# Three values before the first gates, ten gates beside the block solve, and the decay rows stored later

## The chip, the cores and the metric

The kernel runs on one core of a Trainium2 chip. The time is the device time of one execution in microseconds. Before the change it was 1307.09 us, the median of 3 runs (1301.83 to 1307.75).

A core has five engines with a queue of instructions each, worked off in order: PE (matrix multiply; its weight loads, PEld, overlap), DVE (vector), ACT (activation functions and copies), POOL (general) and SP, which here only issues DMA transfers. ACT issues transfers too, between its other instructions. PE writes its results to PSUM, a small memory of banks, from which ACT or DVE must drain them.

## The reference

One layer of a generator over 256 latent tokens with a prefix of 256 context tokens, width 1024: a half-step FFN, a token mixer, another half-step FFN, a norm. All is float32. The mixer runs two scans in both directions over one normalised input:

```
qkv, za, a, beta, zb, xbc, dt, gates = split(h @ w_in)
q, k, v = silu(conv(qkv));  q, k = l2norm(q), l2norm(k)
gated delta scan (8 heads, chunks of 64), per chunk:
    g = cumsum(log a);  decay = exp(g_i - g_j)
    A = strict_lower((k*beta) k^T * decay) + I;  solve A [u, w] = [v*beta, k*beta*exp(g)]
    o = (q exp(g)) S + (q k^T * decay) (u - w S);  S is updated with (u - w S)
SSD scan (32 heads), per chunk:
    a_cs = cumsum(dt * a_neg);  seg = exp(a_cs_l - a_cs_s), lower part
    y = (C B^T * seg) (x*dt) + C S exp(a_cs);  S is updated
merged = sigmoid(ga) * (ya @ w_branch_gdn) + sigmoid(gb) * (yb @ w_branch_mb)
x = x + m5 * (merged @ w_out)
```

Below, a *key* is one head's slice of k, a *value* one of v, and a *gate* one of 16 tiles of `gates` (ga and gb). The *decay rows* are the a_cs of the SSD scan, laid out as rows.

## The kernel before, in words

**Projections.** A projection in full precision splits its weights: `unit` (L185) loads a 128x1024 tile `raw` (issued on SP, L191), ACT casts it to the high part `whi` (L197), DVE subtracts to get the low part `wlo` (L201), and `mm3` issues three matmuls for each of 8 slices (L212 to L214). Keys and values go this way, with 512 columns (context and latent). Gates need less: `projf` (L643) loads `raw` (L638), and PE multiplies straight from it with 256 latent columns (L648, each issued as two matmuls). Line 27 sets the buffers: four of `raw`, three each of `whi` and `wlo`.

**What follows a projection.** A key or a value goes through `conv_silu` (L651): ACT drains the accumulator into a padded buffer `cbuf` (two, shared by keys and values, L659 to L662) and makes the centre tap (L665), DVE adds the four other taps (L667), ACT takes tanh (L670), DVE finishes (L672). A value is then transposed (L1066), drained by ACT (L1068) and stored (L1069). A key is normalised (`l2`, L919), stored, multiplied with itself (L960) and the product stored as `Gsd` (L963); after keys 1, 3, 5 and 7 its diagonal 32x32 blocks are loaded as `N` (L969, on SP). A gate is drained by one tanh on ACT (L1183) and stored (L1184).

**The solve.** `block_decay` and `row_scale` make the decay factors `D` of the blocks. `elim` (L1041) multiplies `N` by `D` (L1045) and then inverts all 32x32 blocks at once in 30 dependent steps of two DVE instructions each (L1049, L1052). Result and transposed copy (L1058) go to DRAM, and `merge` (L1187) reads them back to build the inverses of whole 128-row tiles on PE, for the chain of scan steps.

**The decay rows.** `dts` (L870) computes the steps dt and their running sums `gc` for the SSD scan, and at its end transposes `gc` (L914), negates it on ACT (L916) and stores the rows as `asd` (L917). The SSD scan's diagonal part (`ssd_diag`, L1471) later loads eight rows at a time, broadcast to 128 partitions (`Es`, L1484, 512 KB each), POOL adds the columns (L1497), and DVE and ACT go on from there.

**Who sets the order.** The parts of the mixer are generators, and `PLAN` (L31) lists which are advanced and by how much. `k6` advances the keys by six, `v2` the values by two, `g5` the gates by five; a word alone calls the method of that name. A number before a slash sets the class from that item on: a lower class is earlier. Classes count up from that number with each instruction, so an item that sets 18 again starts beside the first one that did. A planner then simulates the engines and fills each queue by class among what it believes ready, so an instruction of a late class can stand early where nothing better is ready. Weight loads have a class of their own, earlier than all others, and go in program order.

The two keys 0 and 1 and the small projection for a, beta and dt are multiplied before `PLAN` begins. The merges, the chain's steps, the queries (`q`), the SSD inputs (`x`), the sixteenth gate, the `z` projections and the SSD scan come after what is changed.

Of the kernel before, what the change touches and what calls it, by code (L numbers as in the profile page):

```python
# [27 lines left out]
TAGS = dict(tA=4, tS=3, tL=2, tM=2, tZ=2)  # L28
T4 = 2
NCV = 2  # L30
PLAN = """10/k3 block_decay k6 18/g5 13/dts 20/v2 g3 row_scale 5/elim 20/g7 v7 21/gdn_rows 13/m0 14/m1 13/chain_start s0 s1 m2 m3 22/q9  # L31
    B_part 27/x17 25/lat_h 22/C_part 30/g17 chain_out 13/s2 s3 14/gdn_norm 15/ssd_pre 30/zB1 zA9 zB4 15/h40 51/y0 gdn_out y1 70/mb_out"""
NG = 5
GQ = 0
# [102 lines left out]
class Kernel:  # L137
# [537 lines left out]
    def mixer(self, hg):  # L675
# [29 lines left out]
        self.yb = []  # L705
        for tok in PLAN.split():
            p, _, a = tok.rpartition("/")
# [162 lines left out]
    def dts(self):  # L870

        nc, V = self.nc, self.nc.vector
        C = self.const
        mm = nc.tensor.matmul
        x = self.t2([P, 4, 64], "dtx", tag="tZ")
        e = self.t2([P, 4, 64], "dte", tag="tZ")
        z2 = self.t2([P, 4, 64], "dtz", tag="tL")
        V.tensor_copy(x, self.xdt)
        dt = self.dt = self.xdt
        self.softplus(dt, e, z2, x)  # L880
        g = self.t2([P, 4, 64], "dtg", tag="tL")
        V.tensor_tensor(g, dt, self.alog[:, 16:80].rearrange("p (o c) -> p o c", o=1).to_broadcast([P, 4, 64]), op=ALU.mult)
        pc = self.smp([P, 2, 4, 64], "pcd", "mg")
        for d, tri in enumerate((self.UT, self.LT)):
            mm(pc[:, 0, :, 32 * d:32 * d + 32], tri, g[:, :, 32 * d:32 * d + 32], start=True, stop=True)
        mm(pc[:, 1], self.ones, g, start=True, stop=True)
        gc = self.gc = C([P, 4, 64], "gc")
        V.tensor_copy(gc, pc[:, 0])

        gt = pc[:, 1]  # L890
        wc = self.wc = C([P, 2, 2, 32], "wc")
        for j in range(2):
            for d in range(2):
                t = 2 + j
                cs = slice(32 * d, 32 * d + 32)
                w = wc[:, j, d]
                V.tensor_tensor(w, gt[:, t, cs], gc[:, t, cs], op=ALU.subtract)
                if d == j:
                    V.tensor_tensor(w, w, gt[:, 5 - t, cs], op=ALU.add)
        nc.scalar.activation(wc, wc, AF.Exp)  # L900
        wf = wc.rearrange("p a b c -> p a (b c)")
        V.tensor_tensor(wf, wf, dt[:, 2:4], op=ALU.mult)

        wl, egm = self.wl, self.egm = C([P, 2, 32], "wl"), C([P, 2, 32], "egm")
        for d in range(2):
            cs = slice(32 * d, 32 * d + 32)
            V.tensor_tensor(wl[:, d], gt[:, d, cs], gc[:, d, cs], op=ALU.subtract)
            V.tensor_copy(egm[:, d], gt[:, d, cs])
        nc.scalar.activation(wl, wl, AF.Exp)
        nc.scalar.activation(egm, egm, AF.Exp)  # L910
        for d in range(2):
            V.tensor_tensor(wl[:, d], wl[:, d], dt[:, d, 32 * d:32 * d + 32], op=ALU.mult)
        pr = self.smp([P, P], "prow", "mg")
        nc.tensor.transpose(pr, gc[:, 0:2].rearrange("p t c -> p (t c)"), self.ident)  # L914
        rw = self.t2([P, P], "rows_a", tag="tL")
        nc.scalar.activation(rw, pr, AF.Copy, scale=-1.0)  # L916
        nc.scalar.dma_start(self.asd, rw)  # L917
# [783 lines left out]
```

## Time and profile before

| | |
|---|---|
| median of the runs | 1307.09 us |
| the profiled execution | 1309.47 us, its span 1307.8 us |
| PE busy | 1257.8 us (96%) |
| DVE busy | 950.8 us (73%) |
| ACT busy | 482.2 us (37%) |
| POOL busy | 96.7 us (7%) |
| mean granted PE clock | 0.973 |
| keys, from 420 to 471 us | PE busy 51.00, DVE 50.26 |
| until the solve, 470 to 514 us | PE busy 38.35, DVE 16.85 |
| the solve, 514 to 585 us | PE busy 68.05, DVE 63.48 |

How to read the rows that follow. All times are in microseconds from the span's start, and only "mean" and the figure after a group's busy time are nanoseconds. A row in order of time gives start, duration, engine, line, operation, output and inputs, how many were merged into the row, and in brackets the time that the engine had been idle and what ended the idle time. A queue's name with a q (SPq, ACTq) marks the issue of a transfer. A row of a stretch gives its length and the busy time of each engine with the count of instructions, then the granted clock of PE, the busy share of the DMA engines, and GB/s. A group row gives the busy time of all instructions of one line, the mean, and the idle time ahead of them.

### The profile page before, as it was taken

The numbers are of one execution on the slowest core, as the hardware profiler recorded it, in microseconds if no ns is written. First come the engines' busy times: TensorE is split into PE (matmuls) and PEld (weight loads), VectorE is DVE, ScalarE is ACT, GpSimd is POOL, SyncE is SP. The second block draws the span as 40 slices with busy tenths as digits, with TensorE's granted clock in tenths as the row PEclk, the third lists the DMA queues.
The fourth block names the chain that finished last, engine by engine and source line by source line (L and its number), as shares of the span: only waits on it lengthen the run. The fifth ranks groups of instructions, "written<-read, shape, count | busy, mean of one in ns | idle before, by whom it ended". The sixth has DMA issues, their size and how long they took to land.

```text
span 1307.8 us, 21034 instructions
## 1 busy us (share of the span) xinstructions
PE 1257.8 (96%) x8042; PEld 1096.2 (84%) x8042; DVE 950.8 (73%) x1748; ACT 482.2 (37%) x919; POOL 96.7 (7%) x119
## 2 busy tenths in 40 slices
PE   9999999999999989987999999999997999999997
PEld 8888888888899878877888899868555999999997
DVE  5997686556568964897669799847896566856655
ACT  4322122212236652254323445421223445633333
POOL 1000000000010131001110211100211002000000
PEclk9999999999999999998889999999987999999998
DMA  9566467547532389648434356568645665655552
GB/s 367 183 212 206 129 221 230 192 147 238 181 123 89 105 220 232 212 145 235 108 103 117 122 177 196 175 194 286 219 168 199 193 201 182 192 192 185 186 179 79
DMA packets 138131, 239.40 MB, mean 183 GB/s; under 512 B 41072, under 2 KB 81456, under 8 KB 137904
## 3 DMA queue, kind: packets, MB, share of 16 engines
q1 hardware_dynamic: 98688, 214.32, 51.5%
q10 hardware_dynamic: 39344, 23.76, 6.1%
q8 instruction: 63, 1.03, 0.3%
q14 instruction: 36, 0.29, 0.1%
HBM read 211.72 MB, written 26.31 MB: 182 GB/s over the span
## 4 chain that ended last, share of the span: by engine, by line
PE 65%; issue 16%; DVE 9%; DMA 8%; ACT 1%; SPq 0%; POOL 0%; ACTq 0%; DVEq 0%; POOLq 0%
PE acc L213 16%; PE acc L212 16%; PE acc L214 16%; PE acc L648 4%; DVE Es L1499 1%; PE pSs L1125 1%; PE acc L1161 1%; PE pada L318 1%; DMA raw<-in_wgs 1%; DVE Es L1510 1%; DVE wlo L201 1%; PE pn L1339 1%; DMA zsc<-zbt 1%; PE pP L1330 1%; DMA Lm<-Gsd 1%
## 5 line engine op out<-in xcount | busy, mean ns | idle before, releaser
L197 ACT CAST whi<-raw 128x1024 fp32r<-128x1024 f32 (+1 forms) x208 | 214.5, 1034 | 460.3 <-PE acc L213 350.8
L213 PE MATMUL acc<-hL,whi 128*128 128x512 f32 (+1 forms) x976 | 346.1, 355 | 0.5 <-DVE hL L468 0.5
L214 PE MATMUL acc<-hH,wlo 128*128 128x512 f32 (+1 forms) x976 | 346.5, 355 | 0.0
L212 PE MATMUL acc<-hH,whi 128*128 128x512 f32 (+1 forms) x976 | 342.4, 357 | 0.8 <-ACT cv L665 0.5
L201 DVE TENSOR_TENSOR wlo<-raw,whi 128x1024 fp32r<-128x1024 f32 (+1 forms) x208 | 249.7, 1202 | 80.0 <-ACT whi L197 78.8
L212 PEld LDWEIGHTS acc<-hH,whi 128*128 128x128 f32 x976 | 187.7, 193 | 24.6 <-ACT cv L665 0.7
L213 PEld LDWEIGHTS acc<-hL,whi 128*128 128x128 f32 x976 | 188.1, 193 | 23.9 <-DVE hL L468 0.9
L214 PEld LDWEIGHTS acc<-hH,wlo 128*128 128x128 f32 x976 | 188.0, 193 | 23.4
L290 DVE CUSTOM_DVE_ANT_0 junk<-wadat,cs 128x1024 f32<-128x1024 f32 x80 | 97.7, 1221 | 44.1 <-DMA wadat<-in_wadaT 43.4
L213 PE MATMUL acc<-aL,whi 128*128 128x256 f32 (+1 forms) x384 | 122.9, 323 | 0.0
L214 PE MATMUL acc<-aH,wlo 128*128 128x256 f32 (+1 forms) x384 | 122.3, 323 | 0.0
L212 PE MATMUL acc<-aH,whi 128*128 128x256 f32 (+1 forms) x384 | 122.2, 323 | 0.0
L667 DVE SCALAR_TENSOR_TENSOR cv<-cbuf,cc,cv 128x512 f32<-128x512 f32 (+1 forms) x144 | 97.5, 688 | 16.8 <-ACT cv L665 15.4
L648 PE MATMUL acc<-hF,raw 128*128 128x256 f32 x416 | 97.2, 390 | 7.0 <-ACT gth L1183 7.0
L648 PEld LDWEIGHTS acc<-hF,raw 128*128 128x128 f32 x416 | 80.7, 197 | 21.0 <-ACT gth L1183 7.6
L213 PEld LDWEIGHTS acc<-aL,whi 128*128 128x128 f32 x384 | 73.0, 190 | 5.6
L214 PEld LDWEIGHTS acc<-aH,wlo 128*128 128x128 f32 x384 | 72.7, 190 | 5.6
L212 PEld LDWEIGHTS acc<-aH,whi 128*128 128x128 f32 x384 | 72.6, 190 | 5.7
L604 DVE SCALAR_TENSOR_TENSOR xl<-acc,hg,xl 128x256 f32<-128x256 f32 x64 | 30.3, 481 | 47.6 <-PE acc L214 47.0
L1161 PE MATMUL acc<-raw,hF 128*128 128x512 f32 x128 | 58.6, 610 | 0.0
L1161 PEld LDWEIGHTS acc<-raw,hF 128*128 128x128 f32 x128 | 24.9, 197 | 30.0 <-issue 29.9
L401 POOL TENSOR_TENSOR sqa<-sqa,sqb 128x256 f32<-128x256 f32 x12 | 11.7, 978 | 454.9 <-ACT sqb L399 451.9
(403 smaller groups left out, 1968.4 us busy)
## 6 DMA issues: line engine op xcount, KB each, us to landing
raw<-in_wgu SPq DMA_DIRECT2D x76, 512.0 KB, 4.2
wadat<-in_wadaT SPq DMA_DIRECT2D x56, 512.0 KB, 4.1
raw<-in_wdn SPq DMA_DIRECT2D x44, 512.0 KB, 3.8
wada<-in_wada SPq DMA_DIRECT2D x16, 512.0 KB, 9.6
raw<-in_wg SPq DMA_DIRECT2D x16, 512.0 KB, 3.7
Es<-asd SPq DMA_DIRECT2D x16, 512.0 KB, 4.7
raw<-in_wxs SPq DMA_DIRECT2D x16, 512.0 KB, 4.3
raw<-in_wzB SPq DMA_DIRECT2D x16, 512.0 KB, 3.8
```

Of the source, the lines that this page charges most:

```text
L197: nc.scalar.copy(hi, raw)
L201: engs[i % len(engs)].tensor_tensor(lo[:, c:c + w], raw[:, c:c + w], hi[:, c:c + w].bitcast(F32), op=ALU.subtract)
L212: mm(acc, wh, xh, start=start, stop=False)
L213: mm(acc, wh, xl, start=False, stop=False)
L214: mm(acc, wl, xh, start=False, stop=stop)
L290: self.nc.vector.tensor_tensor_reduce(out=self.junk, in0=w, in1=self.cs[s], scale=1.0, scalar=0.0, op0=ALU.mult, op1=ALU.add, accum_out=out)
L318: mm = lambda c, q: nc.tensor.matmul(pa[:, c], loads[k][c][:, q * P:q * P + P], self.cTs[:, q:q + 1].to_broadcast([P, P // 2, 2]), start=q ...
L604: nc.vector.scalar_tensor_tensor(out=xs, in0=acc[:, NL * s - g0:NL * s - g0 + NL], scalar=hg[s][:, m:m + 1], in1=xs, op0=ALU.mult, op1=ALU ...
L648: self.nc.tensor.matmul(acc, w[:, k * P:k * P + P], self.hF[:, k], start=k == 0, stop=k == KD - 1)
L667: nc.vector.scalar_tensor_tensor(out=u3, in0=buf[:, 0:R, j:j + 64], scalar=cw[:, j:j + 1], in1=u3, op0=ALU.mult, op1=ALU.add)
L1125: nc.tensor.matmul(pS[:, d], self.Btok[:, j, m // 8], w[:, d, j], start=j == 0, stop=j == 1)
L1161: nc.tensor.matmul(accs[t], self.hF[:, k, sl], w[:, wsl], start=k == 0, stop=k == 7)
```

## The change

Two things are edited. `PLAN` orders the middle of the mixer anew: three values come before the first gates instead of five gates; two gates, two values and three gates follow; beside the solve come ten gates and three values (the `v4` also ends the generator) instead of seven gates and six values. And the end of `dts`, which transposes and stores the decay rows, becomes a method `dts_rows` of its own, which `PLAN` calls after the values, in the class of `gdn_rows`.

```
-PLAN = """10/k3 block_decay k6 18/g5 13/dts 20/v2 g3 row_scale 5/elim 20/g7 v7 21/gdn_rows 13/m0 14/m1 ...
+PLAN = """10/k3 block_decay k6 18/v3 13/dts 18/g2 20/v2 g3 row_scale 5/elim 20/g10 v4 21/gdn_rows dts_rows 13/m0 14/m1 ...
...
         for d in range(2):
             V.tensor_tensor(wl[:, d], wl[:, d], dt[:, d, 32 * d:32 * d + 32], op=ALU.mult)
+
+    def dts_rows(self):
+
+        nc = self.nc
         pr = self.smp([P, P], "prow", "mg")
-        nc.tensor.transpose(pr, gc[:, 0:2].rearrange("p t c -> p (t c)"), self.ident)
+        nc.tensor.transpose(pr, self.gc[:, 0:2].rearrange("p t c -> p (t c)"), self.ident)
         rw = self.t2([P, P], "rows_a", tag="tL")
         nc.scalar.activation(rw, pr, AF.Copy, scale=-1.0)
         nc.scalar.dma_start(self.asd, rw)
```

More of the change, by code (lines that the diff above doesn't have):

```diff
@@ L30 @@
 NCV = 2
-PLAN = """10/k3 block_decay k6 18/g5 13/dts 20/v2 g3 row_scale 5/elim 20/g7 v7 21/gdn_rows 13/m0 14/m1 13/chain_start s0 s1 m2 m3 22/q9
+PLAN = """10/k3 block_decay k6 18/v3 13/dts 18/g2 20/v2 g3 row_scale 5/elim 20/g10 v4 21/gdn_rows dts_rows 13/m0 14/m1 13/chain_start s0 s1 m2 m3 22/q9
     B_part 27/x17 25/lat_h 22/C_part 30/g17 chain_out 13/s2 s3 14/gdn_norm 15/ssd_pre 30/zB1 zA9 zB4 15/h40 51/y0 gdn_out y1 70/mb_out"""
```

## Prediction

> **What bounds the kernel now.** I read the totals first, then the busy time by stretch around the edited part of the mixer, then the instructions in order of time on each queue there.
>
> ```profile
> span 1307.8 us, 21034 instructions
> PE 1257.8 (96%) x8042; PEld 1096.2 (84%) x8042; DVE 950.8 (73%) x1748; ACT 482.2 (37%) x919; POOL 96.7 (7%) x119
> ...
> core 0: us, PE busy (x) PEld busy (x) DVE busy (x) ACT busy (x) POOL busy (x), PEclk, DMA share, GB/s
> 420.00:471.00 51.00, 51.00 (x276) 44.04 (x275) 50.26 (x111) 29.94 (x104) 14.43 (x17) 1.00 0.43 122
> 470.00:514.00 44.00, 38.35 (x191) 33.01 (x190) 16.85 (x34) 15.31 (x46) 8.88 (x13) 0.92 0.99 231
> 514.00:585.00 71.00, 68.05 (x338) 58.34 (x336) 63.48 (x106) 28.10 (x56) 0.00 (x0) 1.00 0.57 179
> ```
>
> PE bounds the whole, so an edit that reorders work can only remove PE's holes and the slow clock behind them. The three stretches are the key stage, the wait for the solve, and the 32-block solve. DVE is full in the first (50.26 of 51 us), idle for 27 of 44 us in the second, and nearly full again in the third, while the DMA engines are fullest in the second. Work that needs DVE therefore sits in the wrong place. The hole of the second stretch:
>
> ```profile
> 418.25 21.84 SPq L638 DMA_DIRECT2D raw<-in_wg  x4
> 467.70 0.33 SPq L191 DMA_DIRECT2D raw<-in_wv  x1
> 477.76 1.44 SPq L191 DMA_DIRECT2D raw<-in_wv  x1
> ...
> 484.52 1.04 ACT L197 CAST whi<-raw 128x1024 fp32r<-128x1024 f32 x1 [5.99 <-DMA raw<-in_wv]
> ...
> 485.60 1.23 DVE L201 TENSOR_TENSOR wlo<-raw,whi 128x1024 fp32r<-128x1024 f32 x1 [6.74 <-ACT whi L197]
> 486.74 0.68 DVE L936 TENSOR_TENSOR l2n<-l2t,l2r 128x512 f32<-128x512 f32 x1
> ...
> 486.19 1.22 PE L648 MATMUL acc<-hF,raw 128*128 128x256 f32 x2 [5.65 <-ACT gth L1183]
> ```
>
> Four gate weights fill the four raw slots by 440; PE reads a gate's weight out of its slot, so a slot comes free only when that gate has been multiplied. The weights of the first two values are therefore asked for at 467.70 and 477.76. The second lands late, and its cast heads ACT's queue: behind it stand the gates' drains, for which PE waits 5.65 us, and on DVE the split, with a key's normalisation (486.74) behind it. What a hole costs beside itself:
>
> ```profile
> 486.00:488.00 2.00, 1.81 (x4) 1.51 (x5) 1.97 (x6) 1.54 (x5) 0.00 (x0) 0.50 0.50 154
> 490.00:492.00 2.00, 2.00 (x6) 1.55 (x6) 0.22 (x1) 0.00 (x0) 0.00 (x0) 0.50 1.11 343
> 492.00:494.00 2.00, 2.00 (x11) 1.67 (x10) 0.00 (x0) 0.39 (x1) 0.00 (x0) 1.00 0.63 141
> ...
> 516.00:518.00 2.00, 0.89 (x5) 0.43 (x3) 1.94 (x4) 0.72 (x2) 0.00 (x0) 1.00 0.92 272
> 588.00:590.00 2.00, 2.00 (x10) 2.00 (x11) 1.96 (x5) 1.45 (x4) 0.00 (x0) 0.50 1.03 317
> 590.00:592.00 2.00, 2.00 (x15) 2.00 (x14) 1.96 (x5) 0.00 (x0) 0.00 (x0) 0.75 0.82 243
> 660.00:662.00 2.00, 2.00 (x10) 1.27 (x9) 0.93 (x3) 0.93 (x1) 1.15 (x1) 0.50 0.42 166
> ...
> 518.23 1.13 PE L648 MATMUL acc<-hF,raw 128*128 128x256 f32 x4 [1.34 <-ACT gth L1183]
> 587.83 1.12 PE L1066 MATMUL ptm<-ident,cv 128*128 128x128 f32 x4 [4.44 <-DVE cv L672]
> 597.55 0.47 PE L925 MATMUL l2t<-ident,cv 128*128 128x128 f32 x2 [3.40 <-DVE cv L672]
> 653.52 0.71 PE L1242 MATMUL pTw<-TB,Lm 32*32 32x32 f32 x20 [1.01 <-DMA Lm<-Gsd]
> ```
>
> After the 5.65 us hole the granted clock is 0.50 from 486.2 to 492: half of 5.8, some 3.0 us lost (the 0.92 over the whole stretch of 44 us allows up to 3.5). So hole A costs 8.7 us. The 4.44 us hole (C) is followed by 0.50 and 0.75 in 588 to 592: 1.0 + 0.5 lost, 5.9 in all. The 1.34 us hole (B) left the clock at 1.00.
>
> **The change, part by part.** No instruction is added or taken away: sixteen gates, eight values, one transpose, one drain and one store of the decay rows remain. The prices of what moves:
>
> ```profile
> 420.46 0.39 PE L212 MATMUL acc<-hH,whi 128*128 128x512 f32 x1
> 421.14 0.39 PE L212 MATMUL acc<-hH,whi 128*128 128x512 f32 x1
> ...
> 529.33 0.38 ACT L1183 ACTIVATE gth<-acc 128x256 f32<-128x256 f32 x1 [3.07 <-PE acc L648]
> 532.79 0.38 ACT L1183 ACTIVATE gth<-acc 128x256 f32<-128x256 f32 x1 [3.07 <-PE acc L648]
> ...
> L667 DVE SCALAR_TENSOR_TENSOR cv<-cbuf,cc,cv 128x512 f32<-128x512 f32 x24 | 17.5, 741 | 0.0
> L1052 DVE TENSOR_TENSOR N<-N,etmp 128x60 f32<-128x60 f32 (+14 forms) x30 | 15.0, 501 | 0.7
> L1049 DVE TENSOR_TENSOR etmp<-N 128x60 f32<-128x60 f32 (+14 forms) x30 | 15.0, 499 | 3.0 <-DMA vsc<-vt 2.4
> L201 DVE TENSOR_TENSOR wlo<-raw,whi 128x1024 fp32r<-128x1024 f32 x10 | 12.2, 1218 | 3.6 <-ACT whi L197 3.5
> L672 DVE SCALAR_TENSOR_TENSOR cv<-cv 128x512 f32<-128x512 f32 x5 | 3.4, 682 | 0.0
> ...
> 514.22 2.36 DVE L1045 TENSOR_TENSOR N<-N,D 128x1024 f32<-128x1024 f32 x2 [4.54 <-DMA Lm<-Gsd]
> ...
> 583.37 2.01 DVE L1058 COPY D<-N 128x1024 f32<-128x1024 f32 x2
> ```
>
> Three matmuls of a projection take 0.68 us, so a value takes PE 8 x 0.68 = 5.4 us, and a gate 3.46 us (two drains apart). On DVE a value costs 1.22 + 4 x 0.741 + 0.68 = 4.9 us (6 such values lie in the solve: 24 conv steps, here with the solve's two groups of 30); a gate costs DVE nothing.
>
> *Values ahead of the gates.* Before the solve PE now has five gates, two values and three gates: 8 x 3.46 + 2 x 5.4 = 38.5 us; after, five values and five gates: 44.3 us. A value frees its raw slot as soon as it is cast and split, so the weights of v0 to v4 can be asked for from 418 to about 462, ahead of the full DMA stretch. Hole A goes: -8.7 us. (Bounds: 0, if another load stands in its place, to -8.7; I take the whole, because the cause, slots held by waiting gates, is gone.) What is late next is a drain: v2 needs v0's bank, and v0's drain needs a conv buffer that the keys share. I allow a B-sized hole, +1.3 us (bounds 0 to A's 8.7).
>
> The three splits now stand in the full key stage: 3 x 1.22 = 3.7 us. PE is covered by 16 us of the values' own matmuls; without that cover it is +3.7. The keys slip by it, but DVE no longer waits 6.74 us for the cast, so the solve starts about 3 us earlier.
>
> *Ten gates beside the solve.* Seven gates and six values become ten and three, so DVE has 3 x 4.9 = 14.7 us less between the solve's steps, all of it moved into the 27 idle us. The casts and splits that fall in there fall too; ACT gets three more drains and gsc stores.
>
> *The decay rows.* Moved: one transpose, one drain, ACT's store, and what the store releases: two broadcast loads of 512 KB on SP and two POOL adds.
>
> ```profile
> 493.22 0.86 SPq L1484 DMA_DIRECT2D Es<-asd  x2
> 506.35 1.27 SPq L969 DMA_DIRECT2D N<-Gsd  x2
> ...
> 500.38 1.90 POOL L1497 TENSOR_TENSOR Es<-Es,gc 128x1024 f32<-128x1024 f32 x1 [0.39 <-DMA Es<-asd]
> ...
> 501.01 4.17 DVE L667 SCALAR_TENSOR_TENSOR cv<-cbuf,cc,cv 128x512 f32<-128x512 f32 x4 [10.79 <-ACT cv L665]
> 514.09 0.59 ACT L1068 COPY vt<-ptm 128x512 f32<-128x512 f32 x1 [4.09 <-DMA N<-Gsd]
> ```
>
> The loads leave the queue ahead of the last N load, which lets the solve start; they were issued 13 us ahead of it, so I take 0 (bounds 0 to the 1.9 of one add, which DVE's key steps no longer meet). They land beside the solve instead. The second add covered DVE's four conv steps for 1.3 us (501.01 to 502.28), and these took 4.17 instead of 4 x 0.741 = 3.0: 1.2 lost, about as much as the overlap. Two adds of 1.9 us in the solve then stretch it by up to 3.8 (0 if they miss it); I take 3.8. ACT's 4.09 us behind a transfer is what caused B; with the two loads among the gates' weights I count a second such hole, +1.3 (0 to 8.7).
>
> *The solve's end.* -3 at the start, -14.7 and +3.8 in its length: its last copy ends at 585.4 now (583.37 + 2.01) and at about 571.5 then. PE ran dry at 587.83 - 4.44 = 583.4, with all values multiplied by then, and gets there at 583.4 - 8.7 = 574.7. Now the solve's end lies 2 us behind PE, and DVE's backlog makes hole C; then it lies 3 us ahead. C goes: -5.9 (bounds 0 to -10.8, with the 3.40 us hole and a like 1.5 us of lost clock).
>
> Sum: -8.7 - 5.9 + 1.3 + 1.3 = -12.0. The profiled execution took 1309.5 us (span 1307.8 and 1.7 around it), 2.4 above the median 1307.1. So 1297.5 by its clock, and **1295 us** as a median.
>
> The rows disagree on a short hole: 1.34 us left the clock at 1.00, but behind a hole of 1.01 us at 652.5 it stood at 0.50 as late as 660 to 662; if from 656 on, 3 us. Had both my added holes that price, the sum would be -6 (median 1301). The Trainium skill, "TensorE: Matmul & The Clock Gate", Part 1, lets the gate close only after an idle window of about 3.4 us; by that rule they cost no clock and the sum stays at -12. The 1.34 us hole agrees, the 1.01 us one does not.
>
> **The rivals.** *Given back* (no change). A goes, but the keys, with three splits and three values' conv steps in a full DVE queue, deliver the last N no earlier; PE reaches the end of the values 8.7 us sooner and waits there 8.7 us longer. For it: the last N load, at 506.35, follows a chain through every engine. Against it: the 14.7 us taken out of the solve. Time 1307, within 3.
>
> *DVE's queue in the wrong order* (slower). The planner puts whole values (14.7 us) before the last keys, and a value's split into the solve behind the cast that waits for three more gates. Solve start 514.2 - 6.7 + 14.7 = 522.2; length 71.2 - 14.7 + 3.8 + 3 x 3.46 = 70.7; end 592.9, 7.5 late. With a stretch at half clock, 3.0, this is +10.5: 1309.5 + 10.5 - 2.4 = 1317.6. It decides once the solve ends after 585. For it: DVE full at 420 to 471, and the split at 485.60 that did just this. Against it: the keys have the earlier class (10 against 18).
>
> *More than forecast.* The merges start into filled queues, and the 3.40 us hole goes with C: -8.7 - 10.8 - 4 (hole of 1.01 and its clock) = -23.5, 1284.
>
> *The change does nothing*: the planner could keep the old order, but weights are loaded in program order, so the projections must follow the new one. It counts within "given back".
>
> **How the numbers follow.** Forecast 0.48, more 0.10, given back 0.22, wrong order 0.20. Half a percent, 6.5 us, is about what a measurement here can tell from no change. Faster than 1300.6: forecast and more, 0.58. Within: 0.22. Slower: 0.20. The forecast's own range is 1288 to 1301 (short holes free or dear; C whole or half). For eight in ten I go from just under "more", 1282, to 1316, which leaves out half of the slower case.
>
> **What would show it.** PE's 5.65 us wait for L1183 near 480 is absent and the clock stays at 1.00 there; raw<-in_wv issues five times before 465; the first solve step (L1045) at about 511 and its last copy (L1058) near 571; DVE's busy share in the 44 us before the solve well above 16.85; the two early Es<-asd loads and POOL adds inside the solve. I am wrong if L1045 starts after 514, if a hole of A's size stands at another place before the solve, or if PE's holes after it grow by what was won.

## The result and the profile after

The changed kernel takes **1290.49 us**, the median of 4 runs (1287.69 to 1295.55), against 1306.71 us, the median of 4 runs of the kernel before beside it. The ratio is 0.9886, 95% interval 0.9859 to 0.9914: it is faster by 1.1%, some 15 us. The forecast was 1295 us. Lines behind L913 stand four higher in the changed kernel: the solve is L1049 to L1062, a gate's drain L1187, a value's transpose L1070, the merges' first product L1246. In the kernels that repeat an operation of the solve, lines behind it stand one higher still.

The totals of the changed kernel's page:

```profile
span 1290.3 us, 21033 instructions
PE 1247.7 (97%) x8042; PEld 1088.3 (84%) x8042; DVE 954.3 (74%) x1748; ACT 481.3 (37%) x919; POOL 98.8 (8%) x119
```

PE is busy 10.1 us less than before for the same 8042 matmuls: that is half-speed time that has gone (a mean granted clock of 0.981 instead of 0.973, times some 1250 us of busy time, makes 10). The rest of the 17.5 us between the two spans is idle time. To see where, here are the stretches of the changed kernel, the last three beyond those that the prediction used (columns as there: length, busy time of PE, PEld, DVE, ACT and POOL, granted clock, DMA share, GB/s):

```profile
470.00:514.00 44.00, 42.95 (x226) 36.76 (x224) 30.99 (x59) 20.74 (x60) 7.62 (x12) 1.00 0.89 208
514.00:585.00 71.00, 67.36 (x379) 58.84 (x380) 59.53 (x103) 21.81 (x47) 5.20 (x4) 0.95 0.78 246
480.00:514.00 34.00, 32.95 (x176) 28.35 (x174) 20.99 (x42) 12.98 (x39) 3.01 (x6) 1.00 0.87 216
585.00:640.00 55.00, 51.60 (x642) 47.90 (x640) 47.16 (x101) 22.92 (x46) 6.12 (x13) 0.97 0.58 161
640.00:740.00 100.00, 92.37 (x875) 79.67 (x874) 74.62 (x157) 37.29 (x85) 12.83 (x18) 0.97 0.35 107
```

And the same last three of the kernel before:

```profile
480.00:514.00 34.00, 28.35 (x130) 23.91 (x129) 11.60 (x15) 8.96 (x23) 4.44 (x5) 0.90 1.03 232
585.00:640.00 55.00, 44.00 (x421) 40.41 (x422) 41.95 (x86) 21.05 (x47) 5.05 (x7) 0.81 0.65 188
640.00:740.00 100.00, 97.45 (x1040) 84.24 (x1040) 75.80 (x165) 34.31 (x76) 13.22 (x24) 0.95 0.42 116
```

DVE's 27 idle us before the solve are 13 now. What PE loses in a stretch is its idle time and the part of its busy time that a clock below 1.00 costs (busy x (1 - clock)). The four rows come to 14.8 of the 17.5 us; the work that falls into a stretch is not quite the same in both kernels:

| stretch | before: idle + clock | after: idle + clock | change |
|---|---|---|---|
| 480 to 514 | 5.65 + 2.8 | 1.05 + 0 | -7.4 |
| 514 to 585 | 2.95 + 0 | 3.64 + 3.4 | +4.1 |
| 585 to 640 | 11.00 + 8.4 | 3.40 + 1.5 | -14.5 |
| 640 to 740 | 2.55 + 4.9 | 7.63 + 2.8 | +3.0 |

The largest piece lies where the prediction saw its smaller term, behind the values, not in front of the solve. In the queue of transfers of the changed kernel, the value weights are asked for five times before 465, as foreseen, and the two early `Es` loads follow the last `N` load:

```profile
419.44 14.37 SPq L191 DMA_DIRECT2D raw<-in_wv  x3
...
454.29 0.33 SPq L191 DMA_DIRECT2D raw<-in_wv  x1
...
463.53 0.34 SPq L191 DMA_DIRECT2D raw<-in_wv  x1
...
502.25 1.32 SPq L973 DMA_DIRECT2D N<-Gsd  x2
...
515.81 0.34 SPq L1488 DMA_DIRECT2D Es<-asd  x1
...
516.67 0.42 SPq L1488 DMA_DIRECT2D Es<-asd  x1
```

The solve on DVE, from the product with `D` to the last copy, in order of time:

```profile
508.26 2.36 DVE L1049 TENSOR_TENSOR N<-N,D 128x1024 f32<-128x1024 f32 x2 [5.80 <-DMA Lm<-Gsd]
...
517.71 0.25 DVE L1053 TENSOR_TENSOR etmp<-N 128x60 f32<-128x60 f32 x1
...
520.08 2.12 DVE L1056 TENSOR_TENSOR N<-N,etmp 128x216 f32<-128x216 f32 x1
...
526.93 0.47 DVE L1053 TENSOR_TENSOR etmp<-N 128x300 f32<-128x300 f32 x1 [3.80 <-DMA vsc<-vt]
...
560.11 2.18 DVE L1062 COPY D<-N 128x1024 f32<-128x1024 f32 x2
```

The solve starts 6 us earlier than before (508.26 against 514.22), spends some 7 us mostly on two values that stand ahead of its first step (510.6 to 517.7), and then runs almost bare, but for a 3.80 us wait and three splits. Its last copy ends at 562.3, against 585.4: 23 us earlier. What follows it is the merges. Their first matmul `pTw` is the figure to remember; the row of one line gives the durations in ns, then the first and the last start in us. Of the kernel before, with the first of them in order of time, its wait, and the ten us from there:

```profile
L1242 PE MATMUL pTw<-TB,Lm x256: 185/191/258, 610.9 to 720.5; 32*32 32x32 f32 x128
...
610.89 0.69 PE L1242 MATMUL pTw<-TB,Lm 32*32 32x32 f32 x16 [2.80 <-DVE TB L1230]
...
610.00:620.00 10.00, 8.89 (x119) 8.59 (x121) 9.54 (x23) 3.13 (x8) 0.00 (x0) 0.66 0.68 203
```

And of the changed kernel:

```profile
L1246 PE MATMUL pTw<-TB,Lm x256: 184/191/257, 574.8 to 674.8; 32*32 32x32 f32 x128
```

The merges start 36 us earlier, before the last values are done. So PE has merge work and value work side by side from 575 on, and neither the 4.44 us nor the 3.40 us wait for `cv` (L672) is there any more.

### The profile page after: what moved, and what is told of

Read it like the earlier page. It is cut to its first block, busy times and chain, and to the rows that moved or that the text cites. A ratio compares the mean times of both kernels' runs of the same rounds, so it can differ in the third digit from the quotient of the medians.

```text
span 1290.3 us, 21033 instructions
## 1 busy us (share of the span) xinstructions
PE 1247.7 (97%) x8042; PEld 1088.3 (84%) x8042; DVE 954.3 (74%) x1748; ACT 481.3 (37%) x919; POOL 98.8 (8%) x119
## 4 chain that ended last, share of the span: by engine, by line
PE 61%; issue 16%; DVE 12%; DMA 7%; ACT 2%; SPq 1%; POOL 0%; POOLq 0%; DVEq 0%; ACTq 0%
PE acc L213 16%; PE acc L212 16%; PE acc L214 16%; PE acc L648 3%; DVE wlo L201 1%; DVE cv L667 1%; DVE Es L1503 1%; PE acc L1165 1%; PE pada L318 1%; DVE Es L1514 1%; PE pn L1343 1%; DMA vsc<-vt 1%; DVE N L1056 1%; DVE etmp L1053 1%; DMA raw<-in_wgs 1%
## 5 line engine op out<-in xcount | busy, mean ns | idle before, releaser
L213 PEld LDWEIGHTS acc<-hL,whi 128*128 128x128 f32 x976 | 186.6, 191 | 23.9 <-DVE hL L468 0.9
L648 PE MATMUL acc<-hF,raw 128*128 128x256 f32 x416 | 93.1, 380 | 1.9 <-DMA raw<-in_wg 1.7
```

The costliest lines, as they stand in the source:

```text
L213: mm(acc, wh, xl, start=False, stop=False)
L648: self.nc.tensor.matmul(acc, w[:, k * P:k * P + P], self.hF[:, k], start=k == 0, stop=k == KD - 1)
```

## The experiments

The first four kernels take the change apart, the next four move the values and gates about, and the last four edit the solve's steps alone (the planner then also places other work anew). A shortened `PLAN` stands for each; what it doesn't show is as in the kernel before (first four) or the changed kernel. `dts_rows` is there in all that name it.

**Weights of two values loaded early** (the kernel before, `PLAN` untouched; the raw weights of values 0 and 1 get tiles of their own, so that gates cannot hold their slots):

```
-            acc = self.proj("wv", h, self.hH, self.hL, NT, VL[h % len(VL)])
+            acc = self.proj("wv", h, self.hH, self.hL, NT, VL[h % len(VL)], self.t4 if h < 2 else None)
```

> The kernel before, with one edit: the raw weights of values 0 and 1 are loaded into two tiles of another tag (t4, unused there until 493 us), so that they don't wait for a raw slot that a gate still holds. Plan, rows and everything else as before. Theory 'slots' (the 5.65 us hole at 480 comes from value weights asked for too late): both loads issue before 450, PE's 5.65 us wait for L1183 and the 0.50 clock behind it are gone, the solve starts 4 to 7 us before 514.2, and the time falls by 6 to 10 us, to about 1299. Theory 'placement' (the gain of the change comes from DVE work taken out of the solve): the hole may go, but six values still share DVE with the solve, its last copy ends no earlier than 575, and the time falls by less than 4 us.

Measured: 1299.84 us, ratio 0.9938 (0.9919 to 0.9958). In its trace, PE has no hole from 480 to 514, the solve's product with `D` starts at 508.4, and its last copy ends at 575.3. The holes behind the values are nearly as before:

```profile
577.79 0.97 PE L1066 MATMUL ptm<-ident,cv 128*128 128x128 f32 x4 [4.71 <-DVE cv L672]
...
586.59 0.44 PE L925 MATMUL l2t<-ident,cv 128*128 128x128 f32 x2 [2.31 <-DVE cv L672]
...
600.29 0.69 PE L1242 MATMUL pTw<-TB,Lm 32*32 32x32 f32 x16 [1.72 <-DVE TB L1230]
```

So the late weights did cause hole A, as the prediction argued. But this alone brings 0.6%, and the merges have also moved, from 610.9 to 600.3; which of the two pays is not settled here.

**Only the front of the order** (three values first, then eight gates; seven gates and the other values follow):

```
+PLAN: ... k6 18/v3 13/dts dts_rows 18/g5 20/g3 row_scale 5/elim 20/g7 v6 21/gdn_rows ...
```

> Only the front of the change: three values ahead of the first gates, then five gates and three gates as before; seven gates and five values beside the solve; decay rows stored at the end of dts as before. 'Slots': the hole at 480 is gone and most of the gain is there, 1293 to 1298. 'Placement': five of six values are still beside the solve, it ends about 4 us earlier for that, and the time stays above 1300.

Measured: 1294.13 us, ratio 0.9901 (0.9871 to 0.9930). The solve runs bare: no conv step of a value and four splits stand between its first product and its last copy, which ends at 552.0; the merges start at 567.5. `PLAN` names eight gates ahead of the solve, but in the trace some six are multiplied ahead of its first product and some nine beside it, where the kernel before has seven and eight. So it isn't the gates that moved. The values did: three are transposed by 502, the next one at 558, when the solve is over.

**The whole order, the decay rows at their old place:**

```
+PLAN: ... k6 18/v3 13/dts dts_rows 18/g2 20/v2 g3 row_scale 5/elim 20/g10 v4 21/gdn_rows ...
```

> The new order of values and gates, with the decay rows stored right after dts as before. If the rows' move matters for the last N load (theory 'rows'), the solve starts 1 to 3 us after that of the changed kernel (508.3) and the time is 2 us or more above its 1290.5. If it does not, 1288 to 1293; the two POOL adds then fall before the solve, and the solve step of 2.12 us (L1056 at 520) is back at 0.38.

Measured: 1290.85 us, ratio 0.9887 (0.9863 to 0.9911): the changed kernel's time.

**The decay rows moved, the old order:**

```
+PLAN: ... k6 18/g5 13/dts 20/v2 g3 row_scale 5/elim 20/g7 v7 21/gdn_rows dts_rows ...
```

> The old order of values and gates, with only the decay rows moved behind the values. 'Slots' and 'placement': the holes at 480, 583 and 594 stay, 1303 to 1309. 'Rows': the last N load lands 2 us or more before 513.6 and the time falls by 4 us or more.

Measured: 1306.76 us, ratio 1.0004 (0.9987 to 1.0021). One step of the solve meets a POOL add, here as in the changed kernel, and loses some 1.6 us; the time doesn't move. The order is the whole of the gain, and the rows' move is worth nothing.

**Gates first, but ten gates beside the solve.** Ahead of the solve stand the same five values and five gates as in the changed kernel, only the gates first:

```
+PLAN: ... k6 18/g5 13/dts dts_rows 20/v5 row_scale 5/elim 20/g10 v4 21/gdn_rows ...
```

> Five gates stand first as in the kernel before, then five values, then the solve with ten gates and three values beside it. By the theory that the kind of work beside the solve decides (gates, which cost DVE nothing), the hole of 5.65 us in front of the solve stays, so the solve starts near 513, but its steps run nearly bare and it ends before 570; the hole of 4.4 us behind the values goes: half or more of the whole gain, 1293 to 1300 us. By the rival that the order of the first gates and values decides (weights asked for late), this kernel gains nothing: within 3 us of 1306.5.

Measured: 1305.21 us, ratio 0.9994 (0.9977 to 1.001). My theory of that moment, that the kind of work named beside the solve decides, falls. The groups of DVE instructions between the solve's product with `D` (511.9) and the end of its last copy (596.1) show why:

```profile
L667 DVE SCALAR_TENSOR_TENSOR cv<-cbuf,cc,cv 128x512 f32<-128x512 f32 (+1 forms) x36 | 23.4, 663 | 3.1 <-ACT cv L665 2.8
...
L201 DVE TENSOR_TENSOR wlo<-raw,whi 128x1024 fp32r<-128x1024 f32 x11 | 13.4, 1222 | 0.7 <-ACT whi L197 0.7
```

With the gates multiplied first, most of the DVE work of the five values that follow came after that product: 12 conv steps stand between it and the first step, which is at 530.9, one step waits 6.8 us for a value's store (`vsc<-vt`), and the last copy ends 11 us later than before. In the changed kernel the same window, 508.3 to 562.3, holds six conv steps and four splits (in both windows the last split starts only as the copy ends):

```profile
L201 DVE TENSOR_TENSOR wlo<-raw,whi 128x1024 fp32r<-128x1024 f32 x4 | 4.9, 1223 | 1.3 <-ACT whi L197 1.3
L667 DVE SCALAR_TENSOR_TENSOR cv<-cbuf,cc,cv 128x512 f32<-128x512 f32 x6 | 4.4, 748 | 0.1
```

**Three values first, but values beside the solve:**

```
+PLAN: ... k6 18/v3 13/dts dts_rows 18/g5 20/row_scale 5/elim 20/v6 g10 21/gdn_rows ...
```

> Three values stand first, then five gates, then the solve with the other five values beside it and the ten gates behind them. By the theory that the kind of work beside the solve decides, the early hole of 5.65 us is gone but the values' DVE work interleaves with the solve's steps again, its last copy ends at 575 or later, and the time stays near that of the run with early weights alone (1299.8): 1298 to 1304. By the rival that the early values alone make the gain, it is as fast as the changed kernel: 1289 to 1293.

Measured: 1293.03 us, ratio 0.9911 (0.9889 to 0.9932). This is nearly the whole gain, though 20 conv steps interleave with the solve: its last copy ends at 568.0 and the merges start at 597.3.

**Four values first**, in two forms:

```
+PLAN: ... k6 18/v4 13/dts dts_rows 18/g2 20/v1 g3 row_scale 5/elim 20/g10 v4 21/gdn_rows ...
+PLAN: ... k6 18/v4 13/dts dts_rows 18/g5 row_scale 5/elim 20/g10 v5 21/gdn_rows ...
```

> Four values, two gates, one value and three gates ahead of the solve instead of three values, two gates, two values and three gates; the decay rows at their old place. The same five values and five gates stand ahead of the solve, so by the theory nothing but the placing of one value moves: 1289 to 1293. If the values' DVE work ahead of the solve's first steps (some 9 us in the changed kernel) is what still holds the solve up, one value drained earlier moves its last copy from 562 to some 557, and the time by up to 3 us, to 1287.

> Four values and five gates ahead of the solve, then ten gates, then the last four values: one value fewer is drained ahead of the solve. By the theory that the bare solve makes the gain, the solve starts before 509 and its last copy ends before 556, as in the run whose only edit was the front (552), and the time lies between 1288 and 1293. By the rival that the values drained after the solve now stand in front of the merges, PE waits for the last values' conv steps near 590 and the time is 1294 or more.

Measured: 1296.57 us, ratio 0.9928 (0.9901 to 0.9955), and 1297.96 us, ratio 0.9944 (0.9925 to 0.9962). The first missed what I expected. The second lies in the range of its rival, but its trace shows no wait of PE for a conv step near 590, so the rival's reason isn't shown. Their merges start at 577.1 and 567.7, as early as in the changed kernel, and the profiled executions took 1294.8 and 1293.5 us; but the runs spread from 1289 to 1301 and from 1293 to 1303. An earlier solve (last copy at 552.6 in the second) brings nothing more, and a fourth value first is a loss of some 0.5% whose cause I didn't find (the profiled executions are among the faster of their runs; the interval of the first kernel overlaps that of the changed one, that of the second doesn't).

By now the times seemed to go by the start of the merges, and not by hole A. The last four kernels try to turn that one knob.

**The first operation of each solve step twice, three times, and in every third step twice** (the changed kernel; the product is the same each time):

```
+            for _ in range(2):
                 V.tensor_tensor(tmp, N[:, :, k + 1:32, k:k + 1].to_broadcast([P, 2, nr, k]),
                                 N[:, :, k:k + 1, 0:k].to_broadcast([P, 2, nr, k]), op=ALU.mult)
```

> The changed kernel with the first operation of each of the 30 solve steps issued twice (the same product into the same tile): DVE does 15.1 us more in the solve (30 at a mean of 504 ns), and the solve's last copy should end near 562.3 + 15 = 577 instead of 562. By the theory that the solve's end stopped mattering once it lay ahead of PE's running out of values (595 in the changed kernel), PE fills the time with the last values and the time stays within 4 us of the changed kernel: 1287 to 1295. By the rival that each microsecond of the solve's end is a microsecond of the time, 1302 to 1306.

> As the run with the first operation twice, but three times: 30.2 us more DVE work, the last copy near 592, later than the 585 of the kernel before. By the theory, the merges then start after PE has run out of values and gates, as in the kernel before, and a hole of C's kind with half clock comes back: 1297 to 1305. By the rival that each microsecond of the solve's end counts, 1317 to 1321.

> The changed kernel with the first operation of every third solve step issued twice: 10 x 0.5 = 5 us more DVE work in the solve, from which the solve's last copy and the merges' first matmul come somewhat later than 562 and 574.8. Theory from all runs so far: the time goes by the start of the merges (their first matmul, L1246): flat, 1290 to 1298, as long as it lies before 597, and 0.87 us per us beyond (597 gave 1293, 627 gave 1319). So 1290 to 1298 if that matmul stays before 597. By the rival that every microsecond of DVE work in the solve costs one, 1295 to 1297 with the matmul near 580, and one that is tied to the twofold steps' 1304: a third of 13.4, 4.5, over 1290.5.

Measured: 1304.21 us, ratio 0.9976 (0.9965 to 0.9988); 1318.96 us, 1.0092 (1.0062 to 1.0122); 1289.87 us, 0.9879 (0.9855 to 0.9902). The planner reacts to the longer solve: it puts values between the steps again, so that 15 us of work make the last copy 34 us later (596.4), and 30 us make it 52 us later (614.4). With 5 us the last copy ends at 571.7. The merges' first matmul, with the operation twice:

```profile
L1247 PE MATMUL pTw<-TB,Lm x256: 184/191/257, 610.4 to 713.5; 32*32 32x32 f32 x128
```

three times:

```profile
L1247 PE MATMUL pTw<-TB,Lm x256: 184/191/257, 627.2 to 724.1; 32*32 32x32 f32 x128
```

in every third step twice:

```profile
L1247 PE MATMUL pTw<-TB,Lm x256: 184/191/231, 592.3 to 682.8; 32*32 32x32 f32 x128
```

My theory before these runs, that the slack is large, fell with the first two as far as numbers go: both times lie in the ranges of the rival. That rival, that each microsecond of DVE work costs one, falls with the third, which is as fast as the changed kernel though its merges start 17.5 us later. The start of the merges is free up to 592 and perhaps to 597, and then costs about 0.87 us each, an estimate from two kernels that differ in their order too (from 597.3 and 1293.0 to 627.2 and 1319.0).

The start of the merges is a mark of the loss more than all of its cause. In the threefold kernel PE waits longest ahead of the merges' first matmul, for a drain that itself waits for a solve step:

```profile
608.65 0.58 ACT L1073 COPY vt<-ptm 128x512 f32<-128x512 f32 x1 [11.26 <-DVE N L1057]
...
609.29 1.12 PE L1071 MATMUL ptm<-ident,cv 128*128 128x128 f32 x4 [16.25 <-ACT vt L1073]
```

The solve's `etmp` and a value's `vt` come from the same four buffers (`t2`, tag `tA`, L173). So a value's drain can wait for a solve step, as here, and a solve step for a value's store, as in the 3.80 us wait of the changed kernel. No run gives them buffers of their own, so what this costs stays open.

The twofold kernel also gives an estimate of what hole A is worth by itself. It has the early weights and no hole A, and starts its merges where the kernel before does, at 610. Its stretches:

```profile
480.00:514.00 34.00, 32.43 (x169) 27.84 (x168) 20.12 (x38) 12.01 (x32) 2.15 (x4) 1.00 0.78 198
585.00:640.00 55.00, 40.50 (x410) 36.36 (x408) 41.57 (x95) 21.16 (x47) 5.33 (x9) 0.78 0.54 153
```

PE loses 1.6 us instead of 8.5 in the first, and 14.5 + 8.9 = 23.4 instead of 19.4 in the second. Of 6.9 us won, 4.0 are given back there, and the time falls by 3 us. It is an estimate, because this kernel's order and its solve differ from the kernel before as well.

**The kernel before with solve steps 6 to 25 left out** (20 of the 30 steps are not computed, so the blocks are not inverted; gates, values and weights keep the old order):

```
-        for k in range(1, 31):
+        for k in (1, 2, 3, 4, 5, 26, 27, 28, 29, 30):
```

> The kernel before with solve steps 6 to 25 left out (the blocks are not inverted, so the output is another one): 23 us less DVE work in the solve, while the order of gates and values, and with it the hole of 5.65 us ahead of the solve, stays. By the theory that the time goes by the start of the merges, it starts some 20 us earlier, near 590, and the time falls to the level of the changed kernel, 1290 to 1296, though the hole stays. By the prediction's sum, in which that hole costs 8.7 us of its own, only the hole behind the values goes: 1306.7 - 5.9 = 1301, and 1299 at the lowest with the changed kernel's 1290.5 plus 8.7.

Measured: 1289.08 us, ratio 0.9861 (0.9832 to 0.9890). Hole A is still there, and so is the slow clock behind it, but the merges start at 548.5. In order of time on PE:

```profile
486.18 6.25 PE L648 MATMUL acc<-hF,raw 128*128 128x256 f32 x16 [4.46 <-ACT gth L1183]
```

and the stretches:

```profile
480.00:514.00 34.00, 29.54 (x141) 25.17 (x140) 12.60 (x17) 9.55 (x24) 5.69 (x6) 0.90 0.96 242
585.00:640.00 55.00, 53.11 (x698) 50.19 (x696) 46.70 (x97) 24.93 (x51) 6.56 (x15) 0.97 0.62 171
```

PE loses 4.46 + 3.0 = 7.4 us ahead of the solve, and still the kernel reaches the changed one's time, because it loses 1.89 + 1.6 = 3.5 us from 585 to 640 instead of 19.4. It leaves 23 us of DVE work out, which may help later stretches too, so this run shows that the changed kernel's time can be reached with hole A in place, and doesn't measure what the hole is worth.

**All runs by the start of the merges** (each ratio is to runs of the kernel before on the same chip, so the medians of different kernels compare less well than the ratios):

| kernel | hole A | solve's last copy ends | merges start | median us | ratio to before |
|---|---|---|---|---|---|
| steps 6 to 25 left out | yes | 529.7 | 548.5 | 1289.08 | 0.9861 |
| front only | no | 552.0 | 567.5 | 1294.13 | 0.9901 |
| four first, one value fewer | no | 552.6 | 567.7 | 1297.96 | 0.9944 |
| order only | no | 558.8 | 573.5 | 1290.85 | 0.9887 |
| **changed kernel** | no | 562.3 | 574.8 | 1290.49 | 0.9886 |
| four first | no | 561.8 | 577.1 | 1296.57 | 0.9928 |
| every third step twice | no | 571.7 | 592.3 | 1289.87 | 0.9879 |
| values beside | no | 568.0 | 597.3 | 1293.03 | 0.9911 |
| early weights | no | 575.3 | 600.3 | 1299.84 | 0.9938 |
| steps twice | no | 596.4 | 610.4 | 1304.21 | 0.9976 |
| **kernel before** | yes | 585.4 | 610.9 | 1306.71 | 1 |
| rows only | yes | 586.1 | 611.1 | 1306.76 | 1.0004 |
| gates first, ten beside | yes | 596.1 | 612.1 | 1305.21 | 0.9994 |
| steps three times | no | 614.4 | 627.2 | 1318.96 | 1.0092 |

Around 611, with and without hole A, the times lie within 3 us. Up to 597 they lie from 1289 to 1294, again with and without it, but for the two kernels with four values first. No kernel that computes everything beats the changed one beyond the intervals.

## Why the prediction was right and where it wasn't

The forecast of faster held, and 1295 us lies 4.5 above the median. Its sum was made of the wrong parts, though: one term was too large and another too small, and that they nearly make up for each other is luck.

**Hole A, -8.7.** Its cause was read rightly: weights behind slots that gates hold. The early weights alone take it away, and in the changed kernel the wait for L1183 is gone and the clock is 1.00 from 470 to 514. But as a term it was wrong. It priced a hole on the busiest engine as if whatever PE wins there were kept. With the merges' start unchanged, some 3 us of it were kept (twofold steps). That is the rival called *given back*, and its mechanism is real: PE reaches the end of what it may do sooner and waits there. I take it that it did not decide here only because the solve ended earlier as well.

**Hole C, -5.9.** The right mechanism, mis-sized. PE ran dry of values ahead of the solve's result; with the result earlier, the stretch from 585 to 640 loses 14.5 us less, because the 3.40 us hole, the 2.8 us wait for `TB` and their slow clock go with C. The prediction kept the 3.40 us hole and its slow clock for the upper bound (-10.8) and for the rival *more than forecast*. The wait for `TB` it has nowhere, though with the clock of 0.66 from 610 to 620 it cost about as much as C (2.8 us, and 0.34 x 8.89 = 3.0 us). Against that stand 4.1 and 3.0 us lost anew in the solve and behind 640. The threshold, a solve that is done before PE reaches the end of the values at 574.7, fits the runs: with the last copy at 571.7 (every third step twice) nothing is lost; at 575.3 (early weights) some is. That it fits is luck, because PE did not reach the end of the values then, and the kernel with early weights differs in more than its solve's end.

**The solve's end, forecast 571.5, measured 562.3.** The start was to move by 3 us; the product with `D` moved by 6 (the last keys' transposes slipped by 5.6, from 474.8 to 480.4, more than the 3.7 foreseen, but nothing waited for a cast any more). The first step moved by less than 1 us, because the two values' steps stand in between. The length was mis-sized: the prediction let three values of six stay in the solve (-14.7). From 24 conv steps, 5 final steps and 10 splits there remain 6, 2 and 3. At the rows' durations that is 18 x 0.741 + 3 x 0.682 + 7 x 1.218 = 23.9 us less. DVE's busy time between product and last copy fell by less, from 63.85 to 46.13 us, because the rows of interleaved instructions overlap (a conv step of 0.74 us is followed after 0.66) and because an add stretched one step by 1.7; the length fell by 17.1 us. The planner had put the last values behind the solve's end.

**PE at the end of the values, forecast 574.7.** The last value's transpose is at 595.2, later than before (592.2), because PE does merge work first. The number was wrong, and the sum didn't need it beyond the threshold above.

**The added holes, +1.3 each.** There are two of about that size (1.28 and 1.74), for causes not foreseen: values' conv steps that stand in DVE's queue, and a gate's weight. The holes of the changed kernel in the solve, and the two at the merges' start:

```profile
514.23 0.66 PE L1070 MATMUL ptm<-ident,cv 128*128 128x128 f32 x4 [1.28 <-DVE cv L672]
...
534.49 20.96 PE L648 MATMUL acc<-hF,raw 128*128 128x256 f32 x96 [1.74 <-DMA raw<-in_wg]
...
574.84 0.69 PE L1246 MATMUL pTw<-TB,Lm 32*32 32x32 f32 x16 [0.68 <-DVE TB L1234]
576.53 2.56 PE L1246 MATMUL pTw<-TB,Lm 32*32 32x32 f32 x48 [1.00 <-DVE TB L1234]
```

**The decay rows, 0, and the adds, up to 3.8.** The adds did stretch the solve, by 1.7 us: one step took 2.12 us where its neighbour of the same size takes 0.38, and the other add fell into DVE's 3.80 us wait. The time didn't feel it; the kernel without the move is as fast.

**The slower rival.** It was to decide once the solve ends after 585. The kernels whose solve ends at 596 are not slower (0.9994 and 0.9976), and the one at 614 is (1.0092). So its kind is right, and its threshold came at least 10 us too early.

## What to carry to other kernels

A hole on the engine that bounds the whole is worth its length only if nothing further on makes that engine wait for a chain that didn't move; look first for the next point at which it needs a result from another engine, and price the change by when that result comes. What shortens a serial chain is the other work that stands in its queue between its first and last instruction, so count it there, by line, and don't trust the place where the plan names it. The slack of such a chain can be read with one edit: repeat one of its operations a few times, or leave some out, and see where the time begins to follow.

## What the runs showed of the hardware

**An add on POOL holds up a two-input step on DVE.** In the changed kernel the add starts just ahead of the step:

```profile
520.06 1.90 POOL L1501 TENSOR_TENSOR Es<-Es,gc 128x1024 f32<-128x1024 f32 x1 [3.85 <-DVE etmp L1053]
```

It ends at 521.96, and the step that was issued at 520.08 ends at 522.20. That is 0.24 us behind the add, and its neighbour of the same size takes 0.38, so little or nothing of it was done while the add ran. The same pair is in the kernel with only the front changed (add from 512.91 to 514.81, step from 513.05 to 515.09 instead of the usual 0.43). The Trainium skill, "SBUF — State Buffer", section "SBUF: two separate sides", tells of such an exclusive lock; the trace agrees.

**A short hole can cost clock.** Stretches of 2 us of the changed kernel, and one of its holes in order of time:

```profile
532.00:534.00 2.00, 0.75 (x4) 0.32 (x2) 1.87 (x4) 0.38 (x1) 0.00 (x0) 1.00 1.03 411
534.00:536.00 2.00, 1.51 (x7) 1.38 (x8) 1.91 (x3) 0.00 (x0) 0.00 (x0) 1.00 1.01 405
...
576.00:578.00 2.00, 1.47 (x32) 1.48 (x33) 1.84 (x6) 2.00 (x4) 0.00 (x0) 0.65 0.42 66
578.00:580.00 2.00, 2.00 (x25) 1.94 (x23) 1.93 (x5) 2.00 (x6) 0.00 (x0) 0.50 0.41 63
580.00:582.00 2.00, 2.00 (x12) 2.00 (x11) 1.94 (x5) 1.26 (x3) 0.00 (x0) 0.50 0.43 67
582.00:584.00 2.00, 2.00 (x13) 2.00 (x13) 1.94 (x3) 0.23 (x1) 0.00 (x0) 0.65 0.57 161
...
603.95 2.08 PE L1343 MATMUL pn<-ch,TT 128*128 128x128 f32 x8 [2.35 <-DMA ch<-vsc]
...
604.00:606.00 2.00, 2.00 (x9) 2.00 (x10) 1.83 (x4) 1.04 (x3) 0.00 (x0) 0.50 0.48 90
606.00:608.00 2.00, 2.00 (x14) 2.00 (x13) 1.88 (x4) 0.00 (x0) 1.67 (x4) 0.67 0.21 33
```

A single hole of 1.74 us between gates left the clock at 1.00. A single hole of 2.35 us was followed by 0.50 and 0.67. Two holes of 0.68 and 1.00 us with sixteen 32x32 matmuls between them brought it to 0.50 for some 6 us, which is most of the 3.4 us lost to the clock from 514 to 585. But two holes needn't do so: 0.71 and 0.68 us ahead of 128x128 matmuls, at 734.78 and 737.95, left it at 1.00. In the kernel before, a single hole of 1.01 us among 32x32 matmuls was followed by 0.50 from 656 to 662. So the length of a hole alone doesn't tell; whether the small matmuls decide wasn't tried. The Trainium skill, "TensorE: Matmul & The Clock Gate", Part 1, names an idle window of about 3.4 us as what brings the slow clock; these rows show it without one.
